# Twelve small gate tiles carved from six 512-float tiles instead of two 1548-float tiles

## The chip, the cores and the metric

The kernel runs on one core of one Trainium2 chip. The metric is the device time of one execution in microseconds: the time before is a median of 1488.96 us over three runs (1488.23 to 1492.89 us). TensorE (PE) is in-order and its instruction order is written by hand in the kernel (`manual_schedule` for PE only). VectorE (DVE), ScalarE (ACT), GpSimd (POOL) and the DMA queue of SyncE (SP) each run their own instructions in an order that a scheduler fixes at build time.

## The reference, cut to what matters

One layer of a hybrid backbone over 256 context tokens and 512 latent tokens of width 1024. One combined input projection `h @ w_in` feeds three token mixers: SSD (16 heads, here in two groups), mLSTM (4 heads) and GLA (4 heads). Each is a chunked scan in both directions. The three outputs go through their own projections, are gated per channel (`sigmoid(gate) * (y @ w_b)`), summed, projected by `w_out`, and a SwiGLU feed-forward block and a last RMSNorm follow.

```python
lg_f = log_sigmoid(g_af @ gla_a_up[0] + gla_a_bias[0]) / GLA_TAU      # GLA decay
o    = gla_scan(gq, gk, gv, lg_f)  + (the same in the other direction)
dt_f = softplus(s_dtf + ssd_dt_bias[0]);  lf_f = log_sigmoid(m_ff + ml_f_bias[0])
```

SSD and mLSTM need per-token decay sums from `dt` and the forget gates: the "gates' unit" below makes them for both mixers, once, on tiles of 128 x 240 floats (six token chunks of 40 columns).

## The kernel before, in words

Matrix products are done as three products of split operands (high by high, high by low, low by high), so one projection of 128 output channels over 512 tokens is 24 matmuls of 512 columns. Such a projection is a **job**: its weights are loaded (SP, L224), split (a cast on ACT, L216, and a subtraction on DVE or POOL, L218), and its result is drained by what belongs to the job.

The middle of the kernel is one queue of jobs and a list of running **generators**. `PLAN` sets the queue: GLA head 0, GLA head 1, the B and C of SSD, SSD group 0, four projections of the output gates, mLSTM heads 0 and 1, SSD group 1, mLSTM 2 and 3, and so on. After each job every generator is advanced once (by its rate: 1.0 for most, 0.8 for SSD group 1, 0.77 for mLSTM head 2), which writes the next piece of that scan into the PE order. So the scans' small matmuls stand between the projections, and a projection on PE is what covers the chain of DVE, ACT and POOL work that the next scan piece waits for.

Working memory is handed out by **slots** of five classes: `BUFS = dict(t8=3, t6=4, row=8, xk=13, xc=2)`, of 2064, 1548, 1024, 512 and 256 floats a partition. A unit names its need (`Slots(self, need)`), and a job whose need isn't free blocks the queue. While it is blocked, `upcoming` lets through only jobs of the kinds `FILL = ("sz", "mo", "gg", "gate", "wb")`: projections that no scan waits for. Where no filler is left, `jobs` advances the generators with nothing between them (a forced step).

The units that matter here:

- `gates` (L493 on, generator): takes t8=1, row=1 and the tiles in question, and lives for about a dozen advances. It ends with `turn_rows` for mLSTM and gives all its slots back.
- `j_gla(h)`: one decay job with no weights (four small matmuls at L1066 and L1070), then `gqk` (q, k and context k) and three `gv` jobs. Its need is `dict(xk=2, row=2, t6=2, t8=1, xc=1)`; head 0 has its own slots ahead of the queue. `gla_scan` then needs xk=3, row=3, t8=1 more. In it, `pre` makes the decay factors of a level (POOL, ACT, and DVE at L1163) and `products` multiplies on PE (L1173); `turn` transposes (L1205).
- `ssd_scan(g)`: `pre(hl)` for each of eight heads loads rows from DRAM (SP, L774 to L778), does eight tensor_scalars on DVE (L782), an exp on ACT (L784), a multiply on DVE (L785) and an add on POOL (L786). After every second head a **pair** is multiplied on PE (L828, L830), and only then are two of its `row` slots free for `pre` of later heads.
- `ml_scan(h)`: start, an initial state, three steps (L974), four `num` pieces (L991, L992), a normalisation. Its need is row=2, t8=1.

PSUM: five rotating banks for scan pieces ("bank"), three for projections ("acc").

Of the kernel before, what the change touches and what calls it, by code (L numbers as in the profile page):

```python
# [139 lines left out]
class Net:  # L140
# [351 lines left out]
    def gates(self):  # L492
# [3 lines left out]
        own = self.own_gates  # L496
        mC = own.get("xk")[:, :128]
        self.dma(mC, self.a["mC"])
        six = [z[:, 240 * i:240 * i + 240].rearrange("p (i c) -> p i c", c=40)
               for z in (own.get("t6"), own.get("t6")) for i in range(6)]  # L500
        x, u, r, p, laF, laB, la, Pt, tot, g, w = six[:11]
        e = six[11][:, :4]
        t8 = own.get("t8")
# [3 lines left out]
        def take(n, p=128):  # L507
            nonlocal at
            at += n
            return t8[:p, at - n:at]  # L510

        z = take(168)
# [616 lines left out]
    def gla_scan(self, h, own, c9, nt, qk, q2, kc, v, Y):  # L1129
# [85 lines left out]
        def first():  # L1215
            for d in range(2):
# [3 lines left out]
                S.copy(st[:, d, 3 * d], b[:, :256])  # L1220

        side = [lambda: turn(ktc, kw, 0, 4), lambda: turn(ktl, kl, 0, 3), lambda: (turn(ktl, kl, 3, 6), own.put(kl, kw)), first,
                lambda: step(0), lambda: step(1), lambda: step(2)]
        Q = None
# [191 lines left out]
    def startup(self):  # L1416
# [5 lines left out]
        first = [("small",), ("gqk", 0, 0), ("gqk", 0, 1)]  # L1422
        gates = [("gate", b, i, m) for b, i in GATES[:NG] for m in range(2)]
        fetched = iter(gates)

        def load(z):
# [57 lines left out]
        def lat(k):  # L1484
            self.scale_in(x[:, k], TL, 0, k, self.hl[0][k], self.hl[1][k], rbs, EL.split()[k])

        active = iter(gates)
        drained = iter([(0, key) for key in gates])
        for z in STEPS.split():
# [32 lines left out]
            elif z == "D":  # L1522
                for (p, *_), key in zip(groups[3:], gates):
                    self.gate_out(key[1], 2 * key[2] + key[3], p, "sqt")
                    self.release(key)
# [128 lines left out]
    def first(self, Y):  # L1654

        self.own_first = Slots(self, dict(xk=1, row=2, t6=2, t8=1, xc=1))
        jobs = self.j_gla(0, Y)
        q, k = self.gla_q, self.gla_k
        pl, pq, pk = self.groups
        self.gates_need = dict(t6=2, t8=1, row=1, xk=1)  # L1660
        self.own_gates = Slots(self, self.gates_need)
        self.gr = self.own_gates.get("row")
        pc = self.bank()[:, :TX]
        self.dense((pc, self.block(("small",)), 0, 128, self.hx, 0, TX))
        self.release(("small",))
        self.small(pc, 0, 256)
        self.S.copy(self.gr[:48, 256:768], pl[:48])
        self.S.copy(self.gr[:48, :256], pc[:48])
        q(None, pq)
        k(None, pk)  # L1670
        self.release(("gqk", 0, 0))
        self.wtop = BUFS["w"]
        self.wfree = [i for i in self.wfree if i < self.wtop]
        return [jobs[3], jobs[0]] + jobs[4:]
# [364 lines left out]
```

## Time and profile before

| what | value |
| --- | --- |
| median of three runs | 1488.96 us |
| the profiled execution, its own time | 1493.02 us |
| its span, first to last instruction | 1491.2 us |
| PE busy | 1390.2 us (93%) |
| DVE, ACT, POOL busy | 962.1, 670.4, 393.6 us (65%, 45%, 26%) |
| mean granted TensorE clock | 0.970 |
| PE waits named in the trace, the longest | 7.7, 6.7, 6.7, 5.3, 5.3 us by line in total |

PE is busy nearly all the time, and all projections are matmuls at their usual pace. What can move is the remaining idle time of PE, and what a wait does to the granted clock. Rows of the timeline read: start in us, us from first to last of the merged instructions, engine, line, operation, tiles, count, and in brackets the idle time before it and what ended that.

### The profile page before, as it was taken

How to read it: one execution, taken by the hardware profiler on the slowest of the kernel's cores; microseconds unless marked ns; L12 is line 12 of the kernel's file. 1: busy time of each engine (PE TensorE's matmuls, PEld its weight loads, DVE VectorE, ACT ScalarE, POOL GpSimd, SP SyncE). 2: the span in 40 equal slices, each digit the busy share in tenths (PEclk: the TensorE clock that was granted, in tenths of full speed). 3: DMA queues.
4: the chain of work that ended last, by engine and by line, in shares of the span. 5: the costliest groups of instructions: out<-in, count | busy, mean ns of one | idle time of the engine just before them, and what ended most of it. 6: DMA issues, size and time to landing. Idle time of an engine off the chain costs nothing. (4 is left out here: it accounts for less than half of the span.)

```text
span 1491.2 us, 21941 instructions
## 1 busy us (share of the span) xinstructions
PE 1390.2 (93%) x8044; PEld 1194.0 (80%) x8044; DVE 962.1 (65%) x1709; ACT 670.4 (45%) x1254; POOL 393.6 (26%) x345
## 2 busy tenths in 40 slices
PE   5898999999979999998998978999998999999997
PEld 3687879887768887786786867877887999998887
DVE  7957662868494576677675856434438988887332
ACT  4456363553234353333463543333336656566231
POOL 4423522424221212312332706124445000000011
PEclk9999999999999999999999989999999999999998
DMA  7533213142453233236446385656622333324331
GB/s 264 194 107 100 95 56 109 51 124 68 121 148 109 76 93 132 89 101 170 151 154 202 113 261 187 188 176 206 202 78 72 121 107 114 108 91 119 98 91 62
DMA packets 99020, 190.37 MB, mean 128 GB/s; under 512 B 10752, under 2 KB 19472, under 8 KB 97760
## 3 DMA queue, kind: packets, MB, share of 16 engines
q1 hardware_dynamic: 98912, 188.97, 40.8%
q8 instruction: 63, 1.03, 0.3%
q14 instruction: 45, 0.37, 0.1%
HBM read 167.27 MB, written 21.14 MB: 126 GB/s over the span
## 5 line engine op out<-in xcount | busy, mean ns | idle before, releaser
L319 PE MATMUL acc<-hlh,w 128*128 128x512 f32 (+1 forms) x1160 | 388.6, 404 | 6.1 <-ACT w L216 2.0
L216 ACT CAST w<-w 128x512 fp32r<-128x512 f32 (+1 forms) x302 | 182.7, 612 | 377.6 <-DMA w<-in_w_main_dram 172.4
L218 POOL TENSOR_TENSOR w<-w,w 128x512 fp32r<-128x512 f32 x125 | 176.8, 1415 | 541.3 <-ACT w L216 482.4
L218 DVE TENSOR_TENSOR w<-w,w 128x512 fp32r<-128x512 f32 x177 | 136.5, 775 | 210.0 <-ACT w L216 166.5
L319 PEld LDWEIGHTS acc<-hlh,w 128*128 128x128 f32 x1160 | 223.0, 192 | 60.1 <-ACT w L216 2.5
L319 PE MATMUL acc<-hll,w 128*128 128x512 f32 (+1 forms) x576 | 229.4, 398 | 3.7 <-DVE hll L472 1.5
L319 PEld LDWEIGHTS acc<-hll,w 128*128 128x128 f32 x576 | 111.0, 193 | 28.5 <-DVE hll L472 1.9
L319 PE MATMUL acc<-t,w 128*128 128x512 f32 x440 | 115.9, 413 | 7.6 <-ACT t L363 2.9
L319 PEld LDWEIGHTS acc<-t,w 128*128 128x128 f32 x440 | 86.1, 197 | 31.2 <-DVE t L364 4.6
L1809 ACT CAST w<-w 128x512 fp32r<-128x512 f32 x140 | 85.1, 623 | 33.4 <-PE bank L1852 25.7
L1810 DVE TENSOR_TENSOR w<-w,w 128x512 fp32r<-128x512 f32 x140 | 94.9, 688 | 5.0 <-ACT w L1809 4.6
L358 PE MATMUL acc<-w,hlh 128*128 128x256 f32 x512 | 96.9, 289 | 0.1
L1852 PE MATMUL acc<-th,w 128*128 128x256 f32 x480 | 95.3, 281 | 0.2 <-ACT fm L1863 0.2
L1568 POOL TENSOR_TENSOR sq<-sq,sq 128x512 f32<-128x512 f32 x6 | 7.8, 1296 | 307.7 <-ACT sq L1566 307.7
L358 PEld LDWEIGHTS acc<-w,hlh 128*128 128x128 f32 x512 | 81.9, 195 | 3.2 <-issue 1.8
L481 DVE SCALAR_TENSOR_TENSOR cacc<-acc,c_scanc,cacc 128x510 f32<-128x510 f32 (+3 forms) x124 | 77.6, 631 | 5.8 <-ACT cacc L477 5.0
L1852 PEld LDWEIGHTS acc<-th,w 128*128 128x128 f32 x480 | 77.8, 188 | 0.5 <-ACT fm L1863 0.4
L358 PE MATMUL acc<-w,hll 128*128 128x256 f32 x256 | 73.6, 287 | 0.0
L1852 PE MATMUL acc<-tl,w 128*128 128x256 f32 x240 | 67.3, 280 | 0.0
L1411 DVE SCALAR_TENSOR_TENSOR xk<-t 128x1024 bf16<-128x1024 f32 x32 | 42.8, 1337 | 35.6 <-DMA t<-in_wmodT_dram 35.6
L319 PE MATMUL acc<-row,w 128*128 128x512 f32 (+1 forms) x312 | 63.8, 360 | 0.8 <-DVE row L367 0.5
L319 PEld LDWEIGHTS acc<-row,w 128*128 128x128 f32 x312 | 52.1, 188 | 11.2 <-DVE row L367 0.8
(450 smaller groups left out, 2986.6 us busy)
## 6 DMA issues: line engine op xcount, KB each, us to landing
w<-in_w_main_dram SPq DMA_DIRECT2D x180, 256.0 KB, 3.5
w<-in_w_ffs_dram SPq DMA_DIRECT2D x80, 256.0 KB, 2.7
t<-in_wmodT_dram SPq DMA_DIRECT2D x32, 512.0 KB, 4.1
w<-in_w_b_dram SPq DMA_DIRECT2D x48, 256.0 KB, 3.5
xk<-gd SPq DMA_DIRECT2D x40, 256.0 KB, 3.5
w<-in_w_ffo_dram SPq DMA_DIRECT2D x40, 256.0 KB, 2.7
row<-rows SPq DMA_DIRECT2D x16, 512.0 KB, 6.3
wmod<-in_wmod_dram SPq DMA_DIRECT2D x6, 1024.0 KB, 8.6
```

The lines of the kernel that those rows point to most:

```text
L216: self.S.copy(h, w)
L218: self.LE[self.wcount % len(self.LE)].tensor_sub(l, w, h.bitcast(F32))
L319: self.T.matmul(dst, w[:, m0:m1], x[:, c0:c1], start=(k == 0 and j == 0), stop=(k == nk - 1 and j == 2))
L358: self.T.matmul(p, x[:, t0:t0 + 128], w, start=(k == 0 and j == 0), stop=(k == KT - 1 and j == 2))
L481: V.scalar_tensor_tensor(acc[:, o0:o1], p[:, o0 + d:o1 + d], w[:, cc, j:j + 1], acc[:, o0:o1], op0=OP.mult, op1=OP.add)
L1411: V.scalar_tensor_tensor(junk, w, 0.5, sc, op0=OP.mult, op1=OP.mult, accum_out=self.mod[:, 0, j:j + 1])
L1568: self.G.tensor_add(a, a, t)
L1809: S.copy(H, x)
L1810: le[p % 7].tensor_sub(L, x, H.bitcast(F32))
L1852: T.matmul(dst, x, y, start=(first and k == 0 and j == 0), stop=(k == 3 and j == 2), skip_group_check=True)
```

## The change

In `gates` the twelve small tiles of 240 floats came from two `t6` slots, six from each. Now they come from six `xk` slots, two from each (480 of 512 floats). In `first` the need of the unit changes with it: no `t6`, and seven `xk` (one holds the constant mC as before) instead of one. No instruction of the unit changes.

```diff
         six = [z[:, 240 * i:240 * i + 240].rearrange("p (i c) -> p i c", c=40)
-               for z in (own.get("t6"), own.get("t6")) for i in range(6)]
+               for z in [own.get("xk") for _ in range(6)] for i in range(2)]
...
-        self.gates_need = dict(t6=2, t8=1, row=1, xk=1)
+        self.gates_need = dict(t8=1, row=1, xk=7)
```

## Rows read from the trace of the kernel before

**Rows 1.** The page, part 1: engine, busy us, share of span, instructions.
```profile
PE 1390.2 (93%) x8044; PEld 1194.0 (80%) x8044; DVE 962.1 (65%) x1709; ACT 670.4 (45%) x1254; POOL 393.6 (26%) x345
```

**Rows 2.** Stretches: us, busy PE, PEld, DVE, ACT, POOL (counts), PEclk, DMA share, GB/s.
```profile
127.10:350.00 222.90, 215.06 (x1177) 182.52 (x1176) 139.49 (x234) 112.94 (x214) 73.15 (x79) 0.98 0.30 92
350.00:480.00 130.00, 117.43 (x732) 97.72 (x731) 87.67 (x186) 45.30 (x84) 34.58 (x28) 0.96 0.40 111
480.00:590.00 110.00, 110.00 (x548) 91.70 (x546) 66.89 (x140) 49.61 (x89) 22.89 (x18) 1.00 0.34 104
590.00:735.00 145.00, 135.77 (x828) 112.54 (x828) 104.14 (x210) 52.27 (x96) 39.89 (x31) 0.98 0.43 121
```

**Rows 3.** Timeline of PE while the gates' unit runs: the pieces that waited.
```profile
145.74 2.08 PE L1173 MATMUL bank<-row 128*128 128x128 f32 x8 [3.78 <-ACT t L561]
...
187.55 0.60 PE L657 MATMUL bank<-c_ident,t 128*8 128x128 f32 x4 [1.32 <-ACT t L640]
...
192.12 0.49 PE L1066 MATMUL bank<-sm,aup 128*128 128x512 f32 x1 [1.25 <-DVE xk L1177]
```

**Rows 4.** Timeline of ACT ahead of the first of these.
```profile
144.81 0.62 ACT L216 CAST w<-w 128x512 fp32r<-128x512 f32 x1 [2.48 <-DMA w<-in_w_main_dram]
145.33 0.35 ACT L561 COPY t<-bank 128x240 f32<-128x240 f32 x1
```

**Rows 5.** Timeline of PE: the waits around SSD group 0 and mLSTM 0, 1.
```profile
385.58 0.70 PE L966 MATMUL bank<-t,kw 128*128 128x257 f32 x2 [1.45 <-DVE kw L946]
...
423.80 0.70 PE L992 MATMUL bank<-t,row 128*128 128x257 f32 x2 [3.13 <-DVE t L975]
...
442.89 1.12 PE L906 MATMUL bank<-c_ident,xk 128*128 128x128 f32 x4 [4.12 <-DVE xk L834]
```

**Rows 6.** Timeline of PE: the longest wait around SSD group 1.
```profile
700.33 0.47 PE L828 MATMUL bank<-row,t 128*64 128x128 f32 x1 [6.33 <-POOL row L786]
```

**Rows 7.** Stretch after that wait, columns as in rows 2.
```profile
700.00:716.00 16.00, 14.97 (x79) 12.32 (x80) 10.67 (x31) 9.19 (x17) 1.14 (x2) 0.84 0.45 130
```

**Rows 8.** One projection job: PE busy, PEld busy, PEclk of L319 alone.
```profile
127.08:132.69 5.61, 5.61 (x24) 4.33 (x24) 1.00 0.77 234
```

**Rows 9.** Timeline of DVE: the multiply that the first transposes of head 0 read.
```profile
128.79 0.68 DVE L1184 TENSOR_TENSOR xk<-xk,xc 128x512 f32<-128x512 f32 x1
```

**Rows 10.** Timeline of PE: the last matmuls of three SSD pairs.
```profile
418.76 0.41 PE L830 MATMUL bank<-xk,t 128*64 128x128 f32 x3
...
652.41 0.39 PE L830 MATMUL bank<-xk,t 128*64 128x128 f32 x4
...
683.97 0.39 PE L830 MATMUL bank<-xk,t 128*64 128x128 f32 x4
```

**Rows 11.** Timeline of POOL: the add that ends the next pair's chain, for each.
```profile
433.54 1.29 POOL L786 TENSOR_TENSOR row<-row 128x512 f32<-128x512 f32 x1 [7.29 <-ACT w L216]
...
662.61 1.28 POOL L786 TENSOR_TENSOR row<-row 128x512 f32<-128x512 f32 x1 [14.54 <-DVE row L785]
...
698.10 2.17 POOL L786 TENSOR_TENSOR row<-row 128x512 f32<-128x512 f32 x1 [4.05 <-DVE row L785]
```

**Rows 12.** Timeline of PE: token and context jobs, an mLSTM step, a num piece.
```profile
121.32 5.92 PE L358 MATMUL acc<-w,hx 128*128 128x256 f32 x48
...
659.20 1.03 PE L974 MATMUL bank<-t,kw 128*128 128x257 f32 x4
659.88 0.59 PE L358 MATMUL acc<-w,hlh 128*128 128x256 f32 x2
...
684.29 0.70 PE L991 MATMUL bank<-t,row 128*128 128x257 f32 x2
...
685.94 0.58 PE L319 MATMUL acc<-hlh,w 128*128 128x512 f32 x1
```

**Rows 13.** Timeline of DVE: eight tensor_scalars of `pre`, in two places.
```profile
673.99 2.14 DVE L782 TENSOR_SCALAR row<-row,TC,TC 128x128 f32<-128x128 f32 x8 [0.36 <-DMA row<-rows]
...
691.79 3.88 DVE L782 TENSOR_SCALAR row<-row,TC,TC 128x128 f32<-128x128 f32 x8 [1.49 <-DMA row<-rows]
```

## The prediction

> **What bounds the kernel now.** I read the page's busy table first: PE is busy for 1390.2 us of a span of 1491.2 us [rows 1]. The change adds and removes no instruction, so PE's work stays and only its idle time can move. To see where that stands I cut the span by stage. Up to 127 us nothing that the change reorders has reached PE. From 127.1 to 735 us PE is idle for 7.8 us (127 to 350), 12.6 us (350 to 480), none (480 to 590) and 9.2 us (590 to 735), 29.6 us in all [rows 2]. The timeline of PE then gives the single waits: 3.78, 1.32 and 1.25 us while the gates' unit runs [rows 3], 3.13 and 4.12 us around SSD group 0 [rows 5], 6.33 us in SSD group 1 [rows 6]. After a wait the granted clock is often low for some microseconds: 0.84 over the 16 us from 700 [rows 7], that is about 5 us at 1.2 GHz instead of 2.4 and some 2.6 us of lost work on a wait of 6.33. Not every wait is followed by it, so I add a third to a wait for the clock.
>
> The first wait shows what such a wait is made of: PE wants a bank that ACT has to copy out (L561), but ACT stood behind a weight cast that waited 2.48 us for its DMA [rows 4].
>
> **What the change does to the order.** PE's order follows from the free slots, so I replay their count. GLA head 0 holds xk=1, row=2, t6=2, t8=1, xc=1, the gates' unit t6=2, t8=1, row=1, xk=1. That leaves no t6, and head 1 (t6=2) is blocked until the unit ends: seven gate projections run as fillers beside the scan of head 0, then head 1's decay job (in the trace L1066 at 190 to 192 us [rows 3]). After the change the unit holds xk=7 and no t6. When the scan of head 0 has taken xk=3, row=3, t8=1, free are xk=2, row=2, t6=2, t8=1, xc=1: just what head 1 needs. Its decay, gqk (two), context k and three gv jobs come at once, seven jobs earlier, and take the fillers' place between the pieces of the unit and of head 0's scan. Its scan can't follow: it needs row=3 and one row is free until head 0 ends. Five gate jobs fill that time. Head 1's scan then starts four jobs earlier (17th instead of 21st).
>
> Followed on, the queue gives this: SSD group 0 starts its scan three jobs earlier, after six fillers in a row; mLSTM heads 0 and 1 then run as twelve jobs with no filler between them, beside SSD group 0. From there to SSD group 1 sz, mo and gate fillers are plentiful. In SSD group 1 the jobs of mLSTM 2 and 3 stand two places earlier, so five gate fillers instead of three come at its end. From GLA head 2 on (job 92 of 149) the order of jobs is the same, and nine forced steps stand in the queue before and after. So the sum is about 127 to 735 us.
>
> **Stage by stage.** A projection takes 5.6 us of PE [rows 8]; 48 matmuls of 256 columns 5.8 us, so a two-block token job 5.8 and a context job 2.9; an mLSTM step 0.7 (659.20 to 659.88), a num piece 1.65 (684.29 to 685.94) [rows 12].
>
> *Gates' unit, 127 to 200 us.* The 1.25 us wait of head 1's decay behind head 0's products goes (the banks are free when it runs early). The 3.78 us wait lives on a weight DMA that was late; head 1's gv weights are asked for two jobs ahead of their use (three jobs share them), where the gate fillers' were asked for one or two ahead, each anew, so I take 1.0 us to be left (bounds 0 and 3.8). The 1.32 us stays. New: the job ahead of head 0's first transposes was a projection of 5.6 us and is now the decay job, two matmuls of 512 and two of 256 columns, 0.7 us by rows 8. PE is there at 127.8 us, but the multiply it reads ends at 129.47 us [rows 9]: 1.6 us of waiting (up to 4 if DVE drains the decay's four banks first). Head 1's decay brings its DVE work here earlier, but DVE has room between 127 and 350 us (139.5 of 222.9 us [rows 2]). Waits -1.25 - 2.78 + 1.6 = -2.4 us, with the third **-3.2 us**. Bounds: all three waits gone and nothing new, -8.4; the 3.78 us kept and 4 us new, +3.7.
>
> *SSD group 0 with mLSTM 0 and 1.* What decides is the pair chain: from the end of one pair (its row slots free) to the POOL add that the next pair needs, through a DMA, DVE, ACT, DVE and POOL. Measured here: 15.7 us (419.17 to 434.83), 11.1 us (652.80 to 663.89), 15.9 us (684.36 to 700.27) [rows 10, 11]. PE's work between two pairs is the cover. For group 0 it becomes two projections of 5.6 with mLSTM 0's start and initial state between them, 13 or more, then 0.7 + 2.9 + 0.7 + 5.8 = 10.1, then 14.7 us. The second is 2.5 us less than now, but the 3.13 us wait in that place [rows 5] is part of the same leg; at 14.2 us (the mean of the three) PE waits 4.1 us, +1.0. The convolutions of mLSTM 0 now stand beside group 0's states, on DVE, but before mLSTM 0's own scan starts: an estimate of +0.5, a third of the 1.45 us that such a backlog cost there [rows 5]. The 1.45 and 4.12 us waits, both of a backlog on DVE, I leave. **+1.5 us**. Bounds: the 3.13 and 4.12 us gone with a third, -9.7; a chain of 15.9 us and the convolutions doubling the 1.45, +4.2 with a third +5.6.
>
> *SSD group 1 with mLSTM 2 and 3.* First leg: now two token jobs cover it, 12.3 us with the step, over an 11.1 us chain and PE doesn't wait. After the change the token jobs are done: between the pairs stand an mLSTM step, a job that only starts a generator, one num piece and one gate job, 0.7 + 1.65 + 5.6 = 7.9 us. With a chain of 11.1 to 15.9 us PE waits 3.2 to 8.0 us; I take 4.5, near the row of this same leg. Second leg: three gate jobs, no wait. Third leg: one num piece instead of two ahead of the pair that now waits 6.33 us [rows 6], +1.65 at an equal chain; I take +1.2, as DVE has less mLSTM work there. Waits +5.7, with the third **+7.6 us**. Bounds: 3.2 and no more, +4.3 with the third; 8.0 + 1.65, +12.9. Should the chain be much shorter than any measured, the lower bound is 0.
>
> How long the chain is depends on who else is at work: eight tensor_scalars of `pre` took 2.14 us at 674 and 3.88 us at 692 us [rows 13], the latter with POOL splitting weights beside them. The Trainium skill ("SBUF — State Buffer", Who interferes with whom) has it that a tensor_scalar on VectorE in a two-port mode and a GpSimd instruction lock each other out of a shared port; the trace agrees with 1.74 us, and by that rule gate fillers, whose weights POOL helps to split, would lengthen the first leg by as much.
>
> **Sum.** -3.2 + 1.5 + 7.6 = +5.9 us: 1493.0 of the profiled execution (span 1491.2 and 1.8 around it) becomes 1498.9. The profiled execution is 4.1 us over the median of the runs; against that median, 1489.0 + 5.9 = **1494.9 us**.
>
> **Rivals.**
> *Cancelled.* The chain in group 1 takes 11.1 us and leg three doesn't grow (+4.3), group 0 keeps its waits, the unit gains its 3.2: 1490 us. For it: the same fillers and the same nine forced steps. Against it: the leg's cover of 7.9 us is under every chain measured.
> *Faster by mixing.* The unit's waits go entirely (-8.4), and mLSTM 0's convolutions, now spread differently, take DVE's backlog with them (-9.7, rows 5); against group 1's least, +4.3: net -13.8, 1475 us at the most, 1482 if half of it comes. It decides whether DVE keeps up in group 0. For it: 480 to 590 us, rich in fillers, has no idle at all [rows 2]. Against: mLSTM 0 and 1 get no filler at all. The Trainium skill ("Perfetto Trace Analysis", Optimization Strategy) says that interleaving regimes with different contended engines may improve performance; here PE is the busiest in all of them, which speaks for a small effect.
> *It doesn't do what it says.* Head 1 stays blocked by another class, the order is the old one: 1489 us. The slots fit with nothing to spare in xk and row, but they fit.
>
> **How the numbers follow.** What a measurement of this kernel can tell from no change is 0.3%, 4.5 us. Forecast 0.55, of which 0.44 lies above 1493.4 and 0.11 below; cancelled 0.21; mixing 0.21, of which 0.18 is below 1484.5; no new order 0.03. So slower 0.44, the same 0.38, faster 0.18. The forecast's own range is 1490 to 1503 us (+1 to +14: the unit's and group 0's middle with either end of group 1's). For eight in ten it has to reach the cancelled case and half of the mixing: 1482 to 1504 us.
>
> **What would show it.** In the new trace L1066 of head 1 stands right after head 0's last gv job, with a wait of 1 to 4 us at L1205 behind it; the wait at L1173 there is under 2 us. Between the first two pairs of SSD group 1 stands one gate job, and its second pair waits 3 us or more on L786 (the forecast fails if it doesn't); the fourth waits 6 us or more. From GLA head 2 on, PE's idle is within 3 us of before. If that later stretch moves by more, the schedule of the other engines has shifted in a way this sum doesn't hold.

## The result, and the profile after

The changed kernel takes 1498.43 us (median of six runs, 1495.55 to 1505.42), the kernel before 1488.6 us (six runs, 1482.61 to 1492.89): a ratio of 1.0063 [1.0040, 1.0086], 9.8 us slower where +5.9 was forecast. Times and ratios here and below are of fast executions alone: one of e7's six took 7577.93 us and is left out. The profiled execution took 1502.59 us with a span of 1500.8 us, 9.6 us more than before; like that of the kernel before (1493.02 us) it lies some 4 us above its kernel's median. PE's busy time in the page of the kernel after:

```profile
PE 1393.9 (93%) x8044; PEld 1198.8 (80%) x8044; DVE 959.7 (64%) x1709; ACT 668.1 (45%) x1251; POOL 402.0 (27%) x345
```

As many matmuls as in [rows 1], 3.7 us more of busy time at a lower mean clock (0.962 against 0.970), and 106.9 us of idle (1500.8 less 1393.9) against 101.0: 3.7 + 5.9 are the 9.6 us. The stretches of the kernel after, columns as in [rows 2]:

```profile
127.10:350.00 222.90, 218.63 (x1182) 182.62 (x1183) 147.60 (x246) 113.61 (x213) 88.29 (x84) 0.98 0.30 91
350.00:480.00 130.00, 115.77 (x731) 98.66 (x730) 77.58 (x184) 43.68 (x83) 25.70 (x20) 0.93 0.36 103
480.00:590.00 110.00, 107.55 (x539) 89.89 (x538) 67.52 (x137) 46.72 (x87) 21.13 (x16) 0.98 0.33 100
590.00:735.00 145.00, 130.53 (x791) 108.87 (x790) 93.73 (x194) 50.38 (x94) 38.76 (x29) 0.95 0.42 121
```

Where PE is idle longer the granted clock is lower too: 0.93 against 0.96 from 350 us, 0.95 against 0.98 from 590 us. Fixed stretches hold different jobs in the two kernels, so I also added up the bracketed waits between four marks that both have: GLA head 0's decay (the first L1066, at 106.8 us before and 104.9 after), the first L755 of SSD group 0, the first L755 of group 1, and GLA head 2's decay (L1066 or L1070), where the order of jobs is the same again. From head 0's decay to group 0: 8.2 us of idle before, 7.3 after. Group 0 to group 1: 12.6 and 16.6. Group 1 to head 2: 9.2 and 14.4. That is -0.9, +4.0 and +5.2, together +8.3. From head 2's decay to the feed-forward (first L1852) it is 35.1 and 34.5, and ahead of head 0's decay, where nothing changes, 22.9 and 21.3; so some 6 are left of the 8.3, the page's 5.9. Each sum is of one execution.

The 3.7 us of busy time can't be put down to the waits. Between head 0's decay and head 2's, where the waits grew, PE is busy for 614.7 us before and 615.5 after; from there to the feed-forward, where the order is the same, for 364.0 and 367.4 (nine matmuls fall on the other side of the mark). The first experiment below, e1, has PE's order of the kernel before, but for 14 of 8044 places, and 610.2 and 359.7 us: two traces of the old order differ by more.

The timeline of PE after, its waits in the three stages:

```profile
127.29 0.81 PE L1205 MATMUL bank<-c_ident,xk 128*128 128x128 f32 x4 [2.67 <-DVE xk L1184]
140.34 1.15 PE L1173 MATMUL bank<-row 128*128 128x128 f32 x8 [2.32 <-ACT xk L561]
...
353.17 1.94 PE L808 MATMUL bank<-xk,t 128*64 128x512 f32 x2 [2.53 <-DVE xk L767]
...
389.47 1.14 PE L966 MATMUL bank<-t,kw 128*128 128x257 f32 x4 [3.15 <-DVE kw L946]
410.19 1.20 PE L974 MATMUL bank<-t,kw 128*128 128x257 f32 x2 [6.60 <-DVE kw L946]
...
532.84 0.66 PE L727 MATMUL bank<-c_ident,xk 128*128 128x128 f32 x4 [2.45 <-DVE xk L489]
...
667.04 0.47 PE L828 MATMUL bank<-row,t 128*64 128x128 f32 x1 [3.36 <-POOL row L786]
710.08 0.47 PE L828 MATMUL bank<-row,t 128*64 128x128 f32 x1 [9.16 <-POOL row L786]
```

The first wait lies ahead of 127.1 us, outside the stretches. The second is the old 3.78 us wait on L561 [rows 3], but ScalarE no longer stands behind a weight cast there [rows 4]; it works on head 1's decay (L1075, L1076), which now comes early:

```profile
137.85 1.57 ACT L1076 ACTIVATE t<-t,one 128x1536 f32<-128x1536 f32 x1
...
139.85 0.34 ACT L561 COPY xk<-bank 128x240 f32<-128x240 f32 x1
```

The 6.60 us wait stands in group 0's second leg, where 4.1 us were forecast, but at an mLSTM step and not at the pair. VectorE's timeline there:

```profile
405.37 0.35 DVE L782 TENSOR_SCALAR row<-row,TC,TC 128x128 f32<-128x128 f32 x1 [3.18 <-DMA row<-rows]
405.64 0.74 DVE L481 SCALAR_TENSOR_TENSOR cacc<-acc,c_scanc,cacc 128x510 f32<-128x510 f32 x1
...
409.76 0.28 DVE L946 TENSOR_SCALAR kw<-row,TC 128x128 f32<-128x128 f32 x1
```

The step's `kw` (L946) stands in VectorE's order behind the next pair's tensor_scalars (L782), which wait for their row load, and among the pieces of a convolution (L481). The fourth pair of group 1, on PE (the last matmuls of the third pair), SP, DVE and POOL:

```profile
692.62 0.39 PE L830 MATMUL bank<-xk,t 128*64 128x128 f32 x4
...
694.39 0.33 SPq L1279 DMA_DIRECT2D gd<-ctanh  x1
694.81 0.39 SPq L774 DMA_DIRECT2D row<-rows  x1
...
701.29 2.88 DVE L782 TENSOR_SCALAR row<-row,TC,TC 128x128 f32<-128x128 f32 x8 [4.36 <-DMA row<-rows]
...
704.69 0.17 DVE L1023 RECIPROCAL ss<-ss 128x4 f32<-128x4 f32 x1
704.89 1.14 DVE L1025 TENSOR_SCALAR row<-row,ss 128x256 f32<-128x256 f32 x4
705.95 1.22 DVE L978 TENSOR_TENSOR row<-row,xk 128x1024 f32<-128x1024 f32 x1
707.09 1.22 DVE L785 TENSOR_TENSOR row<-row,row 128x1024 f32<-128x1024 f32 x1
...
708.38 1.64 POOL L786 TENSOR_TENSOR row<-row 128x512 f32<-128x512 f32 x1 [6.09 <-DVE row L785]
```

The third pair ended at 693.01 us (692.62 and 0.39), so the chain to the end of the add took 17.0 us; 15.9 was the longest before, in the same place [rows 10, 11]. The row load went out 1.8 us after the pair's end, right behind the gates' store (L1279), where it had been 0.4 us. The multiply L785 started 2.9 us after the tensor_scalars ended, behind mLSTM's norm (L1023, L1025) and L978 on VectorE; ScalarE's exp (L784) had ended at 705.26 us. In the kernel before it had been 1.1 us, right after the exp:

```profile
696.79 1.23 DVE L785 TENSOR_TENSOR row<-row,row 128x1024 f32<-128x1024 f32 x1 [0.52 <-ACT row L784]
```

These two add 3.2 us. The tensor_scalars were 1.0 us shorter (2.88 us, 3.88 before [rows 13]), the load's landing, L785 and the add together 1.1 us.

### The profile page after: what moved, and what is told of

It is laid out like the page before. It is cut to its first block, busy times and chain, and to the rows that moved or that the text cites. A ratio compares the mean times of both kernels' runs of the same rounds, so it can differ in the third digit from the quotient of the medians.

```text
span 1500.8 us, 21953 instructions
## 1 busy us (share of the span) xinstructions
PE 1393.9 (93%) x8044; PEld 1198.8 (80%) x8044; DVE 959.7 (64%) x1709; ACT 668.1 (45%) x1251; POOL 402.0 (27%) x345
## 5 line engine op out<-in xcount | busy, mean ns | idle before, releaser
L319 PE MATMUL acc<-hlh,w 128*128 128x512 f32 (+1 forms) x1160 | 390.4, 406 | 3.8 <-ACT hlh L466 1.9
L218 POOL TENSOR_TENSOR w<-w,w 128x512 fp32r<-128x512 f32 x125 | 174.2, 1394 | 551.8 <-ACT w L216 491.2
L319 PEld LDWEIGHTS acc<-hlh,w 128*128 128x128 f32 x1160 | 224.9, 194 | 57.8 <-ACT hlh L466 2.2
L218 DVE TENSOR_TENSOR w<-w,w 128x512 fp32r<-128x512 f32 x177 | 137.7, 781 | 196.1 <-ACT w L216 165.1
L319 PE MATMUL acc<-hll,w 128*128 128x512 f32 (+1 forms) x576 | 230.7, 400 | 3.7 <-DVE hll L472 1.6
L319 PEld LDWEIGHTS acc<-hll,w 128*128 128x128 f32 x576 | 111.9, 194 | 28.9 <-DVE hll L472 2.2
L319 PE MATMUL acc<-t,w 128*128 128x512 f32 x440 | 114.8, 411 | 6.5 <-DVE t L364 2.8
L319 PEld LDWEIGHTS acc<-t,w 128*128 128x128 f32 x440 | 86.2, 197 | 28.7 <-DVE t L364 4.4
L1852 PE MATMUL acc<-th,w 128*128 128x256 f32 x480 | 95.3, 281 | 0.0
L481 DVE SCALAR_TENSOR_TENSOR cacc<-acc,c_scanc,cacc 128x510 f32<-128x510 f32 (+3 forms) x124 | 77.1, 631 | 19.3 <-ACT cacc L477 18.3
L1852 PEld LDWEIGHTS acc<-th,w 128*128 128x128 f32 x480 | 77.8, 188 | 0.3 <-ACT fm L1863 0.2
L1852 PE MATMUL acc<-tl,w 128*128 128x256 f32 x240 | 67.3, 280 | 0.0
L319 PE MATMUL acc<-row,w 128*128 128x512 f32 (+1 forms) x312 | 63.2, 359 | 0.4 <-DVE row L367 0.4
L319 PEld LDWEIGHTS acc<-row,w 128*128 128x128 f32 x312 | 52.1, 188 | 10.1 <-DVE row L367 0.8
```

Of the source, the lines that this page charges most:

```text
L218: self.LE[self.wcount % len(self.LE)].tensor_sub(l, w, h.bitcast(F32))
L319: self.T.matmul(dst, w[:, m0:m1], x[:, c0:c1], start=(k == 0 and j == 0), stop=(k == nk - 1 and j == 2))
L481: V.scalar_tensor_tensor(acc[:, o0:o1], p[:, o0 + d:o1 + d], w[:, cc, j:j + 1], acc[:, o0:o1], op0=OP.mult, op1=OP.add)
L1852: T.matmul(dst, x, y, start=(first and k == 0 and j == 0), stop=(k == 3 and j == 2), skip_group_check=True)
```

## The experiments

There are twelve; a ratio is to the kernel before on the same chip, whose median differs from chip to chip (1486.17 us beside e5 to e8, 1490.49 beside e12). "The changed kernel" is the starting point unless it says otherwise.

**e1: the new tiles in the old order of jobs.** The unit asks for two `t6` that it doesn't use.

```diff
-        self.gates_need = dict(t8=1, row=1, xk=7)
+        self.gates_need = dict(t6=2, t8=1, row=1, xk=7)
```

> The changed kernel, but the gates' unit also holds two t6 slots that it doesn't use. GLA head 1 is then blocked until the unit ends, so the order of jobs is the old one while the twelve tiles lie in xk slots. Theory A (only the order of jobs costs): 1489 us, within 3 us of the kernel before, the waits at L828 of SSD group 1 back to one of about 6 us. Rival B (the tiles in other slots, or the longer hold on xk, cost by themselves): 1495 us or more.

1489.25 us, ratio 0.998 [0.996, 1.000], and the longest wait in group 1 is the old one, as PE's timeline shows:

```profile
695.72 0.47 PE L828 MATMUL bank<-row,t 128*64 128x128 f32 x1 [6.34 <-POOL row L786]
```

The idle time of the three stages is 8.2, 12.5 and 10.4 us, near the kernel before's. The tiles themselves cost nothing that shows; the whole loss is the order of jobs.

**e2, e3, e4: mending SSD group 1 alone.** e2 moves the job that only starts a generator (M) ahead of mLSTM 3, e3 lets mLSTM 2 advance by 1, e4 does both.

```diff
-... s1 m2 m3 M g2 ...      (e2, e4)
+... s1 m2 M m3 g2 ...
-"m2": 0.77                 (e3, e4)
+"m2": 1
```

> The changed kernel with the job that only starts a generator moved ahead of mLSTM head 3 in the plan. Between the first two pairs of SSD group 1 there are then two projections-like jobs again (cover 13.8 us by the job order instead of 7.9); all else in the order of jobs stays. Theory A (PE waits for the pair chain where the cover is short): the wait of 3.4 us at the second pair is gone, the one of 9.2 us at the fourth stays, 1494 us (4 to 5 us less than the changed kernel). Rival C (the chain is set by DVE's backlog, not by the cover): the wait stays or turns up at the next piece, 1498 us.

> The changed kernel with mLSTM head 2 advanced at rate 1 instead of 0.77. Its pieces end earlier, so its head's slots are free and a normal job stands between the third and fourth pair of SSD group 1: covers 8.9, 18.4, 14.6 us by the job order instead of 7.9, 20.1, 7.2. Theory A: the wait of 9.2 us at the fourth pair falls to 2 us or less, the one at the second stays at 2 to 3 us; with the clock 8 to 11 us less, 1488 us. Rival C: mLSTM's work on DVE then meets the pair chains earlier, waits move and 1495 us or more.

> Both edits of the two runs before this one, covers 14.7, 18.4, 14.6 us. Theory A: no wait over 2 us at any pair of SSD group 1; the gains add up, 1484 us, below the kernel before. Rival C: at or above 1492 us.

1501.0 us, 1.0070 [1.0042, 1.0097]; 1501.61 us, 1.0071 [1.0047, 1.0096]; 1503.55 us, 1.0092 [1.0063, 1.0122]. Three misses. The pair waits did go where their legs got more cover (e3's second pair still waits 2.32 us), but others grew. PE's timeline of e2, at the fourth pair:

```profile
714.71 0.48 PE L828 MATMUL bank<-row,t 128*64 128x128 f32 x1 [16.52 <-POOL row L786]
```

That of e3, at mLSTM 3's start:

```profile
711.22 2.45 PE L966 MATMUL bank<-t,kw 128*128 128x257 f32 x4 [7.28 <-DVE kw L946]
```

That of e4, at mLSTM 3's start:

```profile
710.50 2.45 PE L966 MATMUL bank<-t,kw 128*128 128x257 f32 x4 [10.70 <-DVE kw L946]
```

Group 1's stage has 20.0, 12.2 and 13.7 us of idle (14.4 in the changed kernel), and behind head 2's decay it is 36.5, 40.6 and 40.7 us (34.5).

It isn't cover that is missing at e2's fourth pair: PE has 8.3 us of work there between the third pair's end (689.92 us) and the wait, 7.9 in the changed kernel. The chain is 24.7 us long, as SP issues the row load 9.7 us after the pair's end, behind a store of the gates, whose tanh stood behind a cast on ScalarE that waited for its weights. ACT and SP of e2:

```profile
698.09 0.62 ACT L216 CAST w<-w 128x512 fp32r<-128x512 f32 x1 [4.10 <-DMA w<-in_w_main_dram]
...
699.23 0.33 SPq L1279 DMA_DIRECT2D gd<-ctanh  x1
699.65 0.39 SPq L774 DMA_DIRECT2D row<-rows  x1
```

In e3 and e4 the last pair's row load goes out 4.3 and 9.2 us after the pair's end, and mLSTM 3's `kw` stands on VectorE behind the tensor_scalars that wait for it. So these three don't refute the cover theory for the legs that they mend; what came back hangs, by their traces, on the queue that the next three experiments are about. The remedies of e2 to e4 together with e7's weren't run.

**e5, e6, e7: is it SP's queue?** In the changed kernel the rows of the last pair are loaded right behind a store. e5 issues the row loads from ScalarE's queue, e6 does the same in the kernel before, e7 moves only the store.

```diff
-            self.dma(E.rearrange("p d i t -> p d (i t)"), ...)     (e5, e6; L777 and L778 alike)
+            self.S.dma_start(E.rearrange("p d i t -> p d (i t)"), ...)
-        self.dma(self.gd[b][:, j], t)                              (e7)
+        self.S.dma_start(self.gd[b][:, j], t)
```

> The changed kernel with the pair chain's row loads (L774, L777, L778) issued from ScalarE's queue instead of SyncE's; same jobs, same order. Theory Q (queue): in the changed kernel part of the two long waits is not lack of cover but the row loads standing in SyncE's in-order queue behind the fillers' weight loads and stores (issued 399.46 and 401.98 us in group 0, behind a weight load that stood 14.93 us from 383.24; 694.81 in group 1, 1.8 us after the pair's end). With a queue of their own the 6.60 us wait at L974 falls to 3 us or less, the 9.16 us wait at L828 to 6.5 to 7.5, time 1491 to 1495 us. Rival C (cover alone): both waits stay within 1 us, time 1497 to 1500. Rival P (the issuing costs): ScalarE stands at the row loads until the slots are free, with weight casts behind them; new waits at projections (L319, L358) behind L216, time 1500 or more.

> The same edit on the kernel before. Theory Q: there the last pair's loads go out only 0.4 us after the store ahead of them, and no weight load stands long in front, so its 6.33 us wait stays within 1 us; time 1487 to 1491 us. Rival C: the same here. Rival P: slower by the cost of issuing alone, 1492 or more; the difference between this run and the kernel before is then to be taken off the run before this one.

> The changed kernel with only the gates' stores (L1279) issued from ScalarE's queue, where the tanh that they store has just ended. Theory Q, narrow form: it is the store that holds the row loads in group 1 (store 694.39, row load 694.81, pair's end 693.05), so the 9.16 us wait falls by 1 to 1.8 us, and group 0's 6.60 us stays (weight loads stand there, no store): time 1495 to 1498 us. Rival: the weight loads hold it as well, nothing moves, 1498 plus or minus 1.5.

e5: 1509.21 us, 1.0136 [1.0116, 1.0156]; e6: 1499.8 us, 1.0081 [1.0060, 1.0103]. Rival P by the times: it costs either kernel about the same. But the waits at projections that it named aren't in e5's three stages, and in e6 the fourth pair's wait rose from 6.33 to 9.75 us (its row load went out 3.7 us after the pair's end), which none of the three had named. In e5 group 0's wait was still 6.02 us, and the fourth pair's rose to 10.58, as the load stood behind ScalarE's casts, one of which waited for its weights:

```profile
705.22 0.62 ACT L216 CAST w<-w 128x512 fp32r<-128x512 f32 x1 [2.39 <-DMA w<-in_w_main_dram]
...
706.71 0.44 ACTq L774 DMA_DIRECT2D row<-rows  x1
```

That is 4.3 us after the pair's end (702.46 us), where SP had taken 1.8. So e5 doesn't show what a free queue would give. e7: 1494.91 us (median of five), 1.0051 [1.0031, 1.0071]. Its row load goes out as the pair ends (691.82 us; the last matmuls end at 692.01), and PE's timeline at the fourth pair shows:

```profile
707.43 0.47 PE L828 MATMUL bank<-row,t 128*64 128x128 f32 x1 [7.51 <-POOL row L786]
```

That is 7.51 us instead of 9.16, and group 0's wait is 6.16: the narrow form of theory Q holds for that one wait. In e9 and e11, which leave the store where it is, the fourth wait is 8.71 and 8.46 us, so 0.7 of the 1.65 us is within what traces differ by. The time is 8.7 us over the kernel before, inside the range that was named (1495 to 1498 over 1488.6), but the intervals of e7 and of the changed kernel overlap, so the time alone doesn't show the gain.

**e8: the last leg alone, in the kernel before.**

```diff
-"m2": 0.77
+"m2": 0.9
```

> The kernel before with mLSTM 2 at 0.9 steps per job instead of 0.77: the first 89 of 149 jobs are as before, and in SSD group 1 the work between pairs becomes 13.7, 16.1 and 7.2 us instead of 12.9, 13.5 and 8.9, the last as in the changed kernel; from then on the jobs are in the changed kernel's order. Cover theory: the fourth pair's wait grows from 6.33 by 1.7 to 3 us, nothing else waits, time 1491 to 1494 us. If what counts is only group 1's first leg and group 0, 1488 to 1491.

1485.41 us, 1.0008 [0.9988, 1.0028]. PE's timeline at the fourth pair:

```profile
697.58 0.48 PE L828 MATMUL bank<-row,t 128*64 128x128 f32 x1 [8.92 <-POOL row L786]
```

The wait grew as the cover theory said, from 6.33 [rows 6] to 8.92 us: 1.7 us less work of PE between the pair's end and the wait, and a chain 0.9 us longer (16.8 us). But the stage's idle grew only from 9.2 to 10.5, and the time can't be told from before's. The term is real, and smaller than what can be measured.

**e9, e10: VectorE's order.** Between two jobs the other generators' pieces are issued ahead of the SSD pair's (e10: in the kernel before).

```diff
-        for e in list(self.gens):
+        for e in sorted(self.gens, key=lambda z: z[0].__name__ == "ssd_scan"):
```

> The changed kernel, with the step of every other generator issued ahead of the SSD scan's step between two jobs (same jobs, same rates): the mLSTM step's vector work then stands ahead of the next pair's eight tensor_scalars (L782), which wait for the row loads, and not behind them. Theory V (VectorE's order): group 0's 6.60 us wait (L974 on kw, L946 at 409.76 us behind L782 that waited 3.18 us for its rows) and the 3.15 us wait at L966 are that order; they fall to 2 us together or less, and as the chain that follows has the full cover of its leg, little comes back at L828: group 0's idle 16.6 to 8 to 11 us, time 1489 to 1494 us. Theory C (conserved): PE waits for the chain of the pair in any case; what leaves L974 returns at L828 within 20 us, group 0's idle stays above 14, time 1496 to 1500 us.

> The same edit on the kernel before. Theory V: there no wait of group 0 is a kw behind a row load (3.13 us at L992 on L975, 4.12 us at L906 on L834, both of a backlog), so half of that at most goes: 1485 to 1490 us, and the distance between the two kernels shrinks from 9 to 5 us or less. Theory C: 1488 to 1491 us, distance unchanged.

e9: 1499.58 us, 1.0088 [1.0063, 1.0114]; e10: 1488.03 us, 1.0008 [0.9990, 1.0026]. PE's timeline of e9 in group 0's stage:

```profile
388.20 0.70 PE L966 MATMUL bank<-t,kw 128*128 128x257 f32 x2 [1.98 <-DVE kw L946]
390.00 0.70 PE L966 MATMUL bank<-t,kw 128*128 128x257 f32 x2 [1.09 <-DVE kw L946]
411.97 0.70 PE L974 MATMUL bank<-t,kw 128*128 128x257 f32 x2 [1.70 <-DVE kw L946]
413.57 0.70 PE L974 MATMUL bank<-t,kw 128*128 128x257 f32 x2 [0.89 <-DVE kw L946]
...
462.89 2.05 PE L966 MATMUL bank<-t,kw 128*128 128x257 f32 x4 [5.83 <-DVE kw L946]
```

At L966 and L974 9.75 us became 5.7, but 5.83 came at mLSTM 1's start (0.89 in the changed kernel). Group 0's stage still has 15.8 us of idle. Theory V is right about what PE waits for at 410 us and wrong about what it costs: theory C, though the waits came back elsewhere than at L828. In the kernel before the edit (e10) changes nothing that can be told; the distance between the two kernels didn't shrink.

**e11: mLSTM's norm one step later.**

```diff
-        yield from self.head_norm(ht, ss)
+        yield
+        next(self.head_norm(ht, ss))
+        yield
```

> The changed kernel with mLSTM's norm (L1022 to L1025) between the two idle steps of its generator and not ahead of them: as many steps, same jobs. In the changed kernel L1023, four L1025 and L978 (2.5 us) stand on VectorE ahead of the last pair's L785 (707.09 us); in the kernel before L785 came before L978. Theory N: they lengthen the pair chain by what they take, so the 9.16 us wait falls by 1.2 to 1.5 us (L1023 and L1025; L978 stays); time 1496 to 1498.5. Rival: the chain is set by its row loads and by ScalarE's exp, the wait falls by less than 0.5 us, or the norm lands elsewhere in the chain; time as it was, 1498.4 plus or minus 1.5.

1500.89 us, 1.0081 [1.0058, 1.0105], the wait 8.46 us. VectorE's timeline shows the norm in the same place (L1025 there is the reciprocal, L1027 the multiplies):

```profile
702.51 3.32 DVE L782 TENSOR_SCALAR row<-row,TC,TC 128x128 f32<-128x128 f32 x8 [3.67 <-DMA row<-rows]
...
706.36 0.16 DVE L1025 RECIPROCAL ss<-ss 128x4 f32<-128x4 f32 x1
706.55 1.14 DVE L1027 TENSOR_SCALAR row<-row,ss 128x256 f32<-128x256 f32 x4
...
708.75 1.22 DVE L785 TENSOR_TENSOR row<-row,row 128x1024 f32<-128x1024 f32 x1
```

The edit didn't take it out of the chain, so theory N stays open.

**e12: the fillers put where the scans need them.** Two of the four forced fillers go between mLSTM 0 and 1, and SSD group 1 advances by 1.

```diff
-... s0 F2 F2 m0 m1 s1 ...
+... s0 F2 m0 F2 m1 s1 ...
-"s1": 0.8
+"s1": 1.0
```

> The changed kernel with two of the four forced fillers put between mLSTM 0 and mLSTM 1 (so that the twelve jobs no longer stand together beside SSD group 0) and SSD group 1 at 1.0 steps per job instead of 0.8. Head 1's jobs stay beside the gates' unit. By the queue's replay the work between pairs becomes 11.8, 15.6 and 11.4 us in group 0 (13.7, 10.1, 14.6 in the changed kernel, 12.6, 11.8, 15.6 in the kernel before) and 12.9, 7.2 and 12.8 us in group 1 (7.9, 20.1, 7.2; 12.9, 13.5, 8.9). Theory M (where the fillers stand): PE's idle in group 0's stage falls from 16.6 to 13 us or less and in group 1's from 14.4 to 10 or less, time 1488 to 1493 us, with the early start of head 1 kept. Theory S (waits move and stay): the two stages together keep 28 us of idle or more against 31.0, time 1496 us or more.

1483.6 us, ratio 0.9951 [0.9932, 0.9970]: theory M, faster than its range and than both kernels. Group 0's stage has 12.0 us of idle, group 1's 8.5 (16.6 and 14.4 in the changed kernel). Its stretches, columns as in [rows 2]:

```profile
350.00:480.00 130.00, 119.44 (x684) 98.48 (x683) 86.22 (x188) 44.88 (x80) 34.34 (x27) 0.96 0.44 125
480.00:590.00 110.00, 108.71 (x547) 89.72 (x546) 67.83 (x132) 50.43 (x90) 22.09 (x17) 1.00 0.35 102
590.00:735.00 145.00, 136.48 (x828) 113.79 (x828) 110.23 (x221) 52.85 (x98) 41.61 (x33) 0.99 0.46 138
```

The longest waits of PE's timeline of e12 in the two stages:

```profile
412.63 1.11 PE L906 MATMUL bank<-c_ident,xk 128*128 128x128 f32 x4 [4.10 <-DVE xk L834]
...
458.51 1.17 PE L966 MATMUL bank<-t,kw 128*128 128x257 f32 x4 [3.62 <-DVE kw L946]
...
662.97 0.32 PE L828 MATMUL bank<-row,t 128*64 128x128 f32 x1 [3.43 <-DMA w<-in_w_main_dram]
```

The clock is back as well: 0.96, 1.00 and 0.99, where the changed kernel has 0.93, 0.98 and 0.95. Head 1's jobs still stand beside the gates' unit, so their early start isn't what costs; where the fillers and group 1's pieces then stand is.

## Why the prediction was right, and which step was too small

The direction, the mechanism and the places held: slower, by longer waits around the two SSD groups. The size, +5.9 against 9.8 [6.0, 12.8], was short, step by step:

- *Gates' unit.* The new wait at L1205 was 2.67 us (1.6 taken, 1 to 4 named). The 1.25 us wait of head 1's decay went. The 3.78 us wait became 2.32, not 1.0, and so missed the mark of 2. The weight cast that stood ahead of L561 on ScalarE is gone, as forecast; but the early decay of head 1 put its own work there (L1075, L1076), which the prediction priced on VectorE alone. In e2, e3, e11 and e12, where head 1's jobs stand in the same place, the wait is 3.84 or 3.85 us. In sum -0.9 us instead of -2.4.
- *Group 0, the step that failed.* "The 1.45 and 4.12 us waits, both of a backlog on DVE, I leave", and 0.5 us for the convolutions: +1.5 in all, measured +4.0. The second leg was seen (4.1 forecast), but it is not the pair that PE waits for there. It is the mLSTM step, whose vector work shares VectorE's order with the pair chain and the convolution: 6.60 us. The start of mLSTM 0 cost 3.15 us where 1.45 stood [rows 5], the products at L808 2.53, SSD group 1's transposes at L727 2.45; the 4.12 us wait was gone. The prediction priced each leg against one chain, and not the twelve mLSTM jobs in a row against VectorE. e12, which breaks that row, brings the stage back to 12.0 us; e9, which only reorders VectorE within it, doesn't.
- *Group 1.* +5.7 forecast, +5.2 measured: the second pair 3.36 us (4.5 taken, 3 or more named), the fourth 9.16 (6.33 + 1.2 taken). The second pair's chain (654.91 to 666.98 us) took 12.1 us where 12.4 was taken; its tensor_scalars took 2.14 us (660.85), so the lengthening by POOL that the prediction held possible in this leg didn't come. The fourth grew by 2.8: 1.7 for the cover, as forecast, and 1.1 for a chain of 17.0 us and not 15.9. The prediction had taken off 0.45 for less mLSTM work on DVE; there was more of it in the chain, and the row load went out later, which e7 undid. That the sum comes so close is partly luck: one pair was priced 1.1 us too high, the other 1.6 too low, and the small waits of the stage fell by 1.0.
- *The clock.* The third on the waits made 1.1 us. The granted clock is lower in the stretches with more idle time, and in e12 it is back where the waits are shorter; but PE's busy time, where a lower clock would have to show, differs by 8.9 us in the two stretches between two traces of the old order (the kernel before and e1). So these runs neither show nor refute the third.
- *From head 2 on* the idle differed by 0.6 us, under the 3 named.
- *The range.* 1490 to 1503 us (+1 to +14) doesn't follow from the terms named for it: the middle of the unit and of group 0 with either end of group 1 gives +2.6 to +11.2. The measured 9.8 lies in both.

Of the rivals, "cancelled" fails on the fourth pair's 9.16 us and on group 0. "Faster by mixing" fails in the place that it named: VectorE doesn't keep up in group 0 when mLSTM 0 and 1 get no filler. With fillers between them (e12) the stage's idle time is back at the old one. "It doesn't do what it says" would look like e1: 1489.25 us and the old waits.

Open: e12 makes two edits, and the split between them rests on the stages of one trace. Whether the kernel before would gain as much from these two edits wasn't tried, so the 0.5% is not shown to come from head 1's early start. Its trace doesn't show where that gain lies: from head 0's decay to head 2's it takes 640.2 us at 28.2 us of idle, the kernel before 644.9 at 30.0, but e1, in the old order, 641.4 at 31.1.

## What to carry to other kernels

When units share a queue, freeing a slot class moves jobs far behind the place of the edit: replay the queue to where its order is the same again, and price each stretch by the fillers that are left in it. Mending one leg moved the waits (e2 to e4, e9); they went when the work that nobody waits for was spread over all the legs (e12). Price a leg by every scan that shares its vector engine, and by what stands ahead of its load on the queue, not by one chain alone: in e2 a store there made a chain of 17.0 us one of 24.7.

## What the runs showed of the hardware

Eight tensor_scalars (L782) took 2.14 us alone and longer the more of them ran beside GpSimd's weight subtractions (L218): 2.88 us at 1.0 us of overlap in the changed kernel (701.29 to 702.29), 3.32 at 1.7 in e11 (702.51 to 704.21), 3.88 at 2.3 in the kernel before (691.79 to 694.05, [rows 13]). That is 0.7 to 0.8 us lost for each microsecond of overlap. In e8 there was none at that place. GpSimd's timelines, L218 in the kernel before, the changed kernel, e11, and then e8:

```profile
691.44 2.61 POOL L218 TENSOR_TENSOR w<-w,w 128x512 fp32r<-128x512 f32 x2 [4.97 <-ACT w L216]
...
699.67 2.62 POOL L218 TENSOR_TENSOR w<-w,w 128x512 fp32r<-128x512 f32 x2 [10.34 <-ACT w L216]
...
701.58 2.63 POOL L218 TENSOR_TENSOR w<-w,w 128x512 fp32r<-128x512 f32 x2 [10.24 <-ACT w L216]
...
686.44 2.61 POOL L218 TENSOR_TENSOR w<-w,w 128x512 fp32r<-128x512 f32 x2 [5.20 <-ACT w L216]
696.26 1.26 POOL L786 TENSOR_TENSOR row<-row 128x512 f32<-128x512 f32 x1 [7.20 <-DVE row L785]
```

VectorE's in e8, with 2.14 us between the two:

```profile
691.69 2.14 DVE L782 TENSOR_SCALAR row<-row,TC,TC 128x128 f32<-128x128 f32 x8 [5.85 <-DMA row<-rows]
```

The Trainium skill ("SBUF — State Buffer", Who interferes with whom) says that a tensor_scalar on VectorE in a two-port mode and a GpSimd instruction lock each other out of a shared port. These four traces agree with it: the time is lost by the overlap, and not by whether fillers are near. That L782 runs in such a mode no run here shows. Beside the pair chain's own add (L786) it is the same: 3.13 us at 1.29 us of overlap in the changed kernel (679.87 us). In all fourteen traces an unbroken group of eight without a GpSimd instruction beside it took 2.12 to 2.15 us.
